# A hybrid streaming-encoder block: part of the depthwise convolution's taps as ScalarE products that accumulating transfers add up

## The chip, the cores and the metric

The kernel runs on one core of one Trainium2 chip. The metric is device time in microseconds (us) of one execution. The kernel before takes 2048.03 us (median of three runs, 2047.39 to 2050.57). One more execution, profiled, took 2048.88 us; the span of its instructions is 2047.1 us. Engines are named as in the profile: PE is TensorE (PEld its weight loads), DVE is VectorE, ACT is ScalarE, POOL is GpSimd, SP is SyncE, which here issues nearly all loads.

## The reference

One layer on a residual stream of 256 tokens by 4096 channels, everything in float32: a projection `xn @ w_in` to 14,336 columns, chunked attention with 16 heads, a Conformer convolution module, gates, an output projection, a gated embedding and a last norm. The change touches the convolution module:

```
u = a * jax.nn.sigmoid(g)
u = jnp.pad(u, ((0, 0), (CONV_K - 1, 0), (0, 0)))          # CONV_K = 31
u = lax.conv_general_dilated(u, w_dw[:, None, :], window_strides=(1,), ...,
                             feature_group_count=CONV_WIDTH) + b_dw
u = jax.nn.silu(layer_norm(u, ln_g, ln_b))
return u @ w_pw + b_pw
```

Each of the 2048 channels has 31 weights of its own. Output token t is the bias plus the sum over k of w[k] times u[t + k - 30].

## The kernel before, in words

**Matrix products.** Both operands of every large product are split into a high and a low part of type fp32r, and three products (high by high, low by high, high by low) are summed in PSUM. A weight tile `wt` holds 128 rows by two runs of 512 columns (512 KB); SP loads it (line 405) into one of five buffers. ACT makes the high part `wh` by a cast (line 204), and DVE then the low part `wl` by a subtraction (line 205); there are three buffers of each. PE multiplies (line 372).

**Units and blocks.** `mixed_product` walks over 16 units of 256 input rows, two weight tiles each; a call with its 16 units is a *block* below. A plain unit has 24 matmuls of 512 columns: 12 for each `wh`/`wl` pair. A unit with a star in the order table uses a seven-product scheme: DVE first forms sums `ua` and `ub` of weight quarters (lines 428 to 433), which ACT and DVE split into `uh` and `ul`; it has 21 matmuls and about three times the DVE work.

**Order of the blocks** (lines 930 to 951): `glu_conv(0)`, `glu_conv(1)`, `keys(0)`, `values(0)`, `attention(0)`, `glu_conv(2)`, `glu_conv(3)`, `keys(1)`, `attention(1)`, `keys(2)`, `layer_norm_swish()`, then two more blocks with the last queries, keys and values. Each `glu_conv(c)` yields one of four channel groups: 512 channels, kept transposed in a tile `uT` of 128 channels by 4 slices by 256 tokens.

**Convolution.** For each group, each of its four slices and each of the 31 taps, one DVE instruction computes `cv = cv + w[k] * (uT shifted)` in place (lines 678 to 685). Tap 30 comes first and also adds the bias; a tap k touches 226 + k tokens. The 124 instructions of a group are put into a queue, `later`. At each unit's end `fill(n)` (lines 182 to 184) takes as many entries from the queue as a table says (`early_fills`, line 325). The queue also holds the layer norm's steps (lines 807 to 822).

**What sets the order.** The recorded order of the program is a priority, not the final order: a scheduler places instructions on each engine as it takes them to be ready, and may move a ready instruction ahead of earlier recorded ones, unless they are pinned (`pin`). Afterwards the order on every engine is fixed: an engine executes its list strictly in that order, and an instruction whose semaphore has not come holds up all behind it on that engine. Tiles of 128 x 4 x 256 floats come from a pool `act` with eight buffers.

Of the kernel before, what the change touches and what calls it, by code (L numbers as in the profile page):

```python
# [10 lines left out]
F32 = mybir.dt.float32  # L11
F32R = mybir.dt.float32r
AF = mybir.ActivationFunctionType
# [12 lines left out]
def hybrid_block(  # L26
# [150 lines left out]
        return [pt[:, i * T : (i + 1) * T] for i in range(len(blocks))]  # L177


    later = deque()  # L180

    def fill(n):
        for _ in range(min(n, len(later))):
            later.popleft()()


    def weight_parts(w, col, k0, kc, tiles=None):
# [134 lines left out]

    valued = units("1 3 5 7 8 0* 9 2* 10 4* 11 6* 12 13 14 15")

    early_fills = (4, 6, 7, 1, 5, 1, 5, 1, 5, 1, 2, 4, 6, 6, 6, 4)
    final = units("1 0* 3 2* 5 4* 6* 7 8* 9 10* 12* 11 13 14 15")
    late = units("1 3 5 7 9 11 13 15 0* 2 4* 6 8* 10* 12 14")

    def mixed_product(
        w, col, lhs, comb, order, on_helpers, ahead=None, fills=(0,), on_begin=None, apart=NB,  # L330
        left=(), begin=None,
    ):

        c = [[ps_acc.tile([P, NB], F32, tag="acc", name=f"acc{h}{j}") for j in range(2)] for h in range(NH)]  # L340
        helper = {}
        begun, ends = set(), {}
        n_left = len(left) // 2
        for n, (_, seven) in enumerate(order[: len(order) - n_left]):
            for name in ("P1", "P5", "P6", "P7", "P2", "P3", "P4") if seven else ("P2", "P3", "P4", "X"):
                ends[name] = n
        banks = {"P2": c[0][0], "P3": c[0][1], "P4": c[1][0], "X": c[1][1]}
        made, held = [], []

        def add_left(h, js, out=None, cols=slice(None)):  # L350


            for m in range(0, len(held), 2):
                for j in js:
                    dst = c[h][j] if out is None else out[:, cols]
                    for i, (kb, (wh, wl)) in enumerate(held[m : m + 2]):
                        xh, xl = block(kb, h)
                        for kind, (a, b) in enumerate(((xh, wh), (xl, wh), (xh, wl))):
                            pin(
                                nc.tensor.matmul(  # L360
                                    dst, a, b[:, j, cols],
                                    start=out is not None and m + i + kind == 0,
                                    stop=m + i + 1 == len(held) and kind == 2,
                                )
                            )

        def add(name, x, w2, n, final, kinds=range(3), then=lambda ins: None):

            for kind in kinds:
                a, b = ((x[0], w2[0]), (x[1], w2[0]), (x[0], w2[1]))[kind]  # L370
                made.append(
                    nc.tensor.matmul(  # L372
                        banks[name], a, b, start=name not in begun,
                        stop=final and ends[name] == n and kind == 2 and not (left and name in "P2 P3 P4"),
                    )
                )
                begun.add(name)
                then(made[-1])

        def block(kb, h):  # L380
            t = lhs[kb // 4]
            return [t[:, kb % 4, q, h * P : (h + 1) * P] for q in range(2)]

        def add_plain(n, k, wh, wl, **kw):
            pair = order[n][0]
            for j in range(2):
                for h in range(NH):
                    name = (("P2", "P3"), ("P4", "X"))[h][j]
                    add(name, block(2 * pair + k, h), (wh[:, j], wl[:, j]), n, k == 1, **kw)

        done, after = 0, ExitStack()
        if begin:
            done, behind = begin(add_plain)
            for ins in behind:
                after.enter_context(tc.issue_after(ins.ins))
        last_seven = max((n for n, (_, seven) in enumerate(order) if seven), default=None)
        for n, (pair, seven) in enumerate(order):
            if n < done:
                continue
            if ahead:  # L400
                ahead(pair)
            wts = []
            for k in range(2):
                wt = wpool.tile([P, 2, NB], F32, tag="w", name="wt")
                nc.sync.dma_start(wt, two_columns(w, 2 * pair + k, col, apart))
                wts.append(wt)
            if n >= len(order) - n_left:
                for k in range(2):
                    tiles = left[2 * (n - len(order) + n_left) + k]
                    held.append((2 * pair + k, parts_of(wts[k], 2, tiles and tiles())[0]))  # L410
                fill(fills[n % len(fills)])
                continue
            if not seven:
                for k in range(2):
                    add_plain(n, k, *parts_of(wts[k], 2)[0])
                fill(fills[n % len(fills)])
                continue
            begins = not helper
            if begins:
                for name in ("P1", "P5", "P7", "P6"):  # L420
                    helper[name] = ps_tmp.tile([P, NB], F32, tag="tmp", name=f"acc_{name}")
                banks.update(helper)
            w0, w1 = wts
            ua = upool.tile([P, 2, NB], F32, tag="u", name="ua")
            ub = upool.tile([P, 2, NB], F32, tag="u", name="ub")
            plus = partial(nc.vector.tensor_tensor, op=ALU.add)
            w0h, w0l = parts_of(w0, 1)[0]
            plus(ua[:, 0], w0[:, 0], w0[:, 1])  # L428
            plus(ua[:, 1], w0[:, 1], w1[:, 1])  # L429
            uah, ual = pair_parts(ua)  # L430
            w1h, w1l = parts_of(w1, 2)[0]
            plus(ub[:, 0], ua[:, 0], w1[:, 1])  # L432
            plus(ub[:, 1], ub[:, 0], w1[:, 0])  # L433
            ubh, ubl = pair_parts(ub)
            first = len(made)

            def s_of(i):
                t, at = comb[pair] if isinstance(comb, dict) else (comb[pair // 4], pair % 4)
                return [t[:, at + i // 2, q, (i % 2) * P : (i % 2 + 1) * P] for q in range(2)]

            k0, k1 = 2 * pair, 2 * pair + 1
            add("P1", block(k0, 0), (w0h[:, 0], w0l[:, 0]), n, True)
            add("P5", s_of(1), (uah[:, 0], ual[:, 0]), n, True)
            add("P7", s_of(0), (uah[:, 1], ual[:, 1]), n, True)
            add("P2", block(k1, 0), (w1h[:, 0], w1l[:, 0]), n, True)
            add("P3", s_of(3), (w1h[:, 1], w1l[:, 1]), n, True)
            add("P6", s_of(2), (ubh[:, 0], ubl[:, 0]), n, True)
            add("P4", block(k1, 1), (ubh[:, 1], ubl[:, 1]), n, True)
            if begins and on_begin:
                on_begin()  # L450
            if begins:
                tc.add_manual_dep(
                    made[first].ins, last_transpose[0].ins.name,
                    mybir.DependencyInfo(mybir.DependencyClass.NoSync, mybir.DependencyReason.DATA),
                    reason="transposes before the helpers take their banks",
                )
            if n == last_seven:
                on_helpers(helper)
            fill(fills[n % len(fills)])
        after.close()  # L460
        return (c, add_left) if left else c

# [210 lines left out]

    conv = []

    def conv_tap(cv, uT, i, b, k):
        if k == PAD:
            nc.vector.tensor_scalar(
# [2 lines left out]
        else:  # L681
            nc.vector.scalar_tensor_tensor(  # L682
                cv[:, i, PAD - k :], uT[:, i, : T + k - PAD], dw[:, b, k : k + 1],
                cv[:, i, PAD - k :], ALU.mult, ALU.add,
            )

    def more_combinations(pair):

# [5 lines left out]
    def glu_conv(c):  # L694
# [4 lines left out]
        else:  # L699
            last = c == CW // NB - 1  # L700
            sg, gate = scaled_pair(
                w_in0, o_a + c * NB, o_g - o_a, early_six if last else early, r_x, early_fills,
                ahead=more_combinations if last else None,
            )
        for h in range(NH):
# [15 lines left out]
            )  # L721
        cv = act.tile([P, 4, T], F32, tag="act", name="cv")
        for i in range(4):
            for k in reversed(range(TAPS)):
                later.append(partial(conv_tap, cv, uT, i, 4 * c + i, k))
        conv.append(cv)


# [185 lines left out]
    def keys(g, fills):  # L914
        q, k = blocks((o_q + g * NB, o_k + g * NB), early, fills)
        queries(g, q)
        keyed(g, k)
# [4 lines left out]
    def late_pool():  # L922
# [13 lines left out]
    glu_conv(2)  # L936
    glu_conv(3)
    load_bias(1)
    keys(1, early_fills)
    attention(1)  # L940
    keys(2, early_fills)
    layer_norm_swish()
    load_bias(2)
    q, vs[2] = blocks((o_q + 3 * NB, o_v + 2 * NB), early, (4,))
    queries(3, q)
    attention(2)
    k, vs[3] = blocks(
        (o_k + 3 * NB, o_v + 3 * NB), valued, (5, 5, 4, 5, 4, 2, 3, 2, 3, 2, 3, 4, 4, 4, 4, 4),
        then=late_pool,
    )  # L950
    keyed(3, k)
# [358 lines left out]
```

## Time and profile before

| | before |
|---|---|
| median of the runs | 2048.03 us |
| profiled execution | 2048.88 us, span 2047.1 us |
| busy share PE / DVE / ACT / POOL | 99% / 95% / 58% / 0% |
| granted TensorE clock, mean | 0.996 |
| DMA traffic | 412.30 MB, mean 201 GB/s |
| convolution's taps (DVE) | from 105.9 us to 805.1 us of the span |

A row of groups reads: line, engine, operation, what it writes and reads, shape and count, then busy time, mean duration in ns, idle time just before. Matmuls are pipelined: the recorded duration of a matmul is longer than its distance to the next one, so a busy PE is not necessarily a PE at its peak. A row of windows gives busy time and count of each engine in a stretch of the span. A row of the chain of waits gives a start, a length and whose work it was.

### The profile page before, as it was taken

Reading aid. Unit: us, or ns where it says so; the run is one execution under the profiler, and the core shown is the slowest. Engines: PE = TensorE matmul, PEld = TensorE weight load, DVE = VectorE, ACT = ScalarE, POOL = GpSimd, SP = SyncE. Lnnn points to the kernel's source line nnn. Section 1 sums busy time; section 2 is a strip of 40 time slices with the busy share of each in tenths; the row PEclk is TensorE's granted clock in tenths of the full one; section 3 lists DMA queues with packets and bytes.
Section 4 is the critical chain, followed back from the end, with each engine's and each line's share of the span. In section 5 each row is a group of like instructions: output and inputs, shape, how many; then the busy total and the mean of one; then the engine's idle time right before and its main releaser. Section 6 shows DMA issues by size and latency. Waiting matters only on the chain.

```text
span 2047.1 us, 26034 instructions
## 1 busy us (share of the span) xinstructions
PE 2022.0 (99%) x9082; PEld 1656.1 (81%) x9082; DVE 1943.8 (95%) x2784; ACT 1195.2 (58%) x1543; POOL 8.1 (0%) x19
## 2 busy tenths in 40 slices
PE   9999999999999999999999999999999999999997
PEld 7888888888778888878888888888888888888876
DVE  7999999989999999889899999999999999999998
ACT  7655545655555544676565656676565666655555
POOL 0000000000000000000000000000000000000000
PEclk9999999999999999999999999999999999999998
DMA  8666666566665666645666666676666656666765
GB/s 288 192 197 205 204 192 200 165 203 185 192 187 170 199 198 183 191 155 199 192 213 210 193 214 200 216 242 208 214 198 206 204 188 208 199 220 205 235 207 179
DMA packets 157758, 412.30 MB, mean 201 GB/s; under 512 B 12974, under 2 KB 16190, under 8 KB 157626
## 3 DMA queue, kind: packets, MB, share of 16 engines
q1 hardware_dynamic: 156976, 409.80, 63.5%
q8 instruction: 71, 1.16, 0.2%
q10 hardware_dynamic: 650, 0.84, 0.1%
q14 instruction: 61, 0.50, 0.1%
HBM read 406.39 MB, written 4.19 MB: 201 GB/s over the span
## 4 chain that ended last, share of the span: by engine, by line
PE 88%; DVE 7%; issue 2%; DMA 1%; ACT 1%; SPq 0%; POOL 0%; POOLq 0%; ACTq 0%; DVEq 0%
PE acc L372 69%; PE acc_P L372 16%; DVE wl L205 2%; DVE cv L682 2%; PE tmp_ps L170 1%; DVE ul L205 1%; PE acc L218 1%; DMA wt<-in_w_in_dram 1%; DVE ub L433 0%; PE tmp_ps L835 0%; PE tmp_ps L851 0%; DVE ub L432 0%; DMA wt<-in_w_out_dram 0%; ACT wh L204 0%; PE tmp_ps L869 0%
## 5 line engine op out<-in xcount | busy, mean ns | idle before, releaser
L372 PE MATMUL acc<-wh,big_t 128*128 128x512 f32 x4196 | 1296.9, 392 | 2.5 <-ACT wh L204 1.0
L204 ACT CAST wh<-wt 128x1024 fp32r<-128x1024 f32 (+1 forms) x737 | 711.1, 976 | 561.0 <-PE acc L372 416.2
L372 PEld LDWEIGHTS acc<-wh,big_t 128*128 128x128 f32 x4196 | 784.9, 188 | 166.3 <-ACT wh L204 1.8
L205 DVE TENSOR_TENSOR wl<-wt,wh 128x1024 fp32r<-128x1024 f32 (+1 forms) x737 | 819.5, 1123 | 36.6 <-ACT wh L204 32.4
L372 PE MATMUL acc<-wl,big_t 128*128 128x512 f32 x2098 | 805.6, 392 | 2.8 <-DVE wl L205 2.7
L372 PEld LDWEIGHTS acc<-wl,big_t 128*128 128x128 f32 x2098 | 393.4, 188 | 87.8 <-DVE wl L205 6.1
L682 DVE SCALAR_TENSOR_TENSOR cv<-uT,dw,cv 128x255 f32<-128x255 f32 (+22 forms) x480 | 212.1, 460 | 1.0
L204 ACT CAST uh<-ub 128x1024 fp32r<-128x1024 f32 x130 | 136.7, 1052 | 114.0 <-DVE ub L433 97.4
L204 ACT CAST uh<-ua 128x1024 fp32r<-128x1024 f32 x130 | 136.9, 1053 | 82.2 <-DVE ua L429 76.5
L205 DVE TENSOR_TENSOR ul<-ub,uh 128x1024 fp32r<-128x1024 f32 x130 | 158.4, 1219 | 7.0 <-ACT uh L204 6.3
L372 PE MATMUL acc_P<-uh,big_t 128*128 128x512 f32 x528 | 161.6, 393 | 0.0
L205 DVE TENSOR_TENSOR ul<-ua,uh 128x1024 fp32r<-128x1024 f32 x130 | 158.3, 1218 | 0.8 <-ACT uh L204 0.2
L372 PEld LDWEIGHTS acc_P<-uh,big_t 128*128 128x128 f32 x528 | 97.4, 188 | 24.3 <-ACT uh L204 5.1
L428 DVE TENSOR_TENSOR ua<-wt 128x512 f32<-128x512 f32 x130 | 89.0, 685 | 18.1 <-DMA wt<-in_w_in_dram 11.4
L372 PE MATMUL acc_P<-ul,big_t 128*128 128x512 f32 x264 | 101.1, 394 | 1.2 <-DVE ul L205 1.2
L429 DVE TENSOR_TENSOR ua<-wt 128x512 f32<-128x512 f32 x130 | 88.7, 683 | 1.8 <-DMA wt<-in_w_in_dram 1.1
L433 DVE TENSOR_TENSOR ub<-ub,wt 128x512 f32<-128x512 f32 x130 | 88.9, 684 | 0.9
L432 DVE TENSOR_TENSOR ub<-ua,wt 128x512 f32<-128x512 f32 x130 | 88.7, 683 | 0.3
L372 PE MATMUL acc<-uh,big_t 128*128 128x512 f32 x260 | 80.6, 390 | 0.0
L372 PE MATMUL acc_P<-wh,big_t 128*128 128x512 f32 x260 | 80.4, 389 | 0.0
L372 PE MATMUL acc_P<-uh,comb_t 128*128 128x512 f32 x228 | 69.8, 391 | 0.1
L372 PEld LDWEIGHTS acc_P<-ul,big_t 128*128 128x128 f32 x264 | 49.2, 188 | 15.2 <-DVE ul L205 5.0
(240 smaller groups left out, 1370.1 us busy)
## 6 DMA issues: line engine op xcount, KB each, us to landing
wt<-in_w_in_dram SPq DMA_DIRECT2D x447, 512.0 KB, 4.2
wt<-in_w_out_dram SPq DMA_DIRECT2D x128, 512.0 KB, 4.1
wt<-in_w_ple_gate_dram SPq DMA_DIRECT2D x128, 512.0 KB, 4.2
wt<-in_w_pw_dram SPq DMA_DIRECT2D x32, 512.0 KB, 4.5
hc<-in_x_dram SPq DMA_DIRECT2D x8, 512.0 KB, 5.8
wt<-in_w_ple_dram SPq DMA_DIRECT2D x8, 512.0 KB, 4.5
xin<-in_x_dram SPq DMA_DIRECT2D x7, 512.0 KB, 7.9
out_dram<-hc SPq DMA_DIRECT2D x12, 256.0 KB, 2.8
```

Of the source, the lines that this page charges most:

```text
L170: nc.tensor.transpose(pt[:, i * T + h * P : i * T + (h + 1) * P], src[:, h, b] if len(src.shape) == 4 else src[:, h, b * P : (b + 1) * P], ...
L204: nc.scalar.copy(wh[:, :kc, :], wt[:, :kc, :]),
L205: nc.vector.tensor_tensor(wl[:, :kc, :], wt[:, :kc, :], wh[:, :kc, :].bitcast(F32), ALU.subtract),
L218: nc.tensor.matmul(acc, a, b[:, k, :], start=kb == 0 and kind == 0, stop=kb == kblocks - 1 and kind == 2,)
L372: nc.tensor.matmul(banks[name], a, b, start=name not in begun, stop=final and ends[name] == n and kind == 2 and not (left and name in "P2 ...
L428: plus(ua[:, 0], w0[:, 0], w0[:, 1])
L429: plus(ua[:, 1], w0[:, 1], w1[:, 1])
L432: plus(ub[:, 0], ua[:, 0], w1[:, 1])
L433: plus(ub[:, 1], ub[:, 0], w1[:, 0])
L682: nc.vector.scalar_tensor_tensor(cv[:, i, PAD - k :], uT[:, i, : T + k - PAD], dw[:, b, k : k + 1], cv[:, i, PAD - k :], ALU.mult, ALU.add,)
```

## The change

For each group the lowest taps (k = 0 to 14 of the first two groups, 0 to 13 of the third, 0 to 9 of the fourth: 54 taps) leave DVE. Such a tap becomes four ACT products, one per slice, from `uT` into a tile `tap`, whose first 30 tokens POOL sets to zero once; then POOL issues one transfer of 512 KB that adds the whole tile onto `cv` (`accum_op=ALU.add`). A group has two `tap` tiles, used in turn. The adds of a group are put into a second queue, `adds`, behind the group's remaining DVE taps; `add_one` takes one of them at two of three units. Those that are left are recorded ahead of `layer_norm_swish`. The tables of `fill` are changed to fit the shorter queue.

```
+    def add_one(n):
+        if adds and n % 3 < 2:
+            adds.popleft()()
...
-    early_fills = (4, 6, 7, 1, 5, 1, 5, 1, 5, 1, 2, 4, 6, 6, 6, 4)
+    early_fills = (4, 5, 5, 1, 4, 1, 4, 1, 4, 1, 2, 3, 4, 4, 4, 3)
+    more_fills = (6, 7, 7, 2, 6, 2, 6, 2, 6, 2, 4, 6, 8, 8, 8, 6)
...
             fill(fills[n % len(fills)])
+            add_one(n)
...
+    ADDED = (15, 15, 14, 10)
+
+    def conv_added(cv, uT, c):
+
+        held = []
+
+        def tap(k):
+            if k < 2:
+                held.append(act.tile([P, 4, T], F32, tag="act", name="tap"))
+                nc.gpsimd.memset(held[k][:, :, :PAD], 0.0)
+            t = held[k % 2]
+            for i in range(4):
+                b = 4 * c + i
+                nc.scalar.activation(
+                    t[:, i, PAD - k :], uT[:, i, : T + k - PAD], AF.Identity,
+                    scale=dw[:, b, k : k + 1],
+                )
+            nc.gpsimd.dma_start(cv, t, accum_op=ALU.add)
+
+        return [partial(tap, k) for k in range(ADDED[c])]
...
         for i in range(4):
-            for k in reversed(range(TAPS)):
+            for k in reversed(range(ADDED[c], TAPS)):
                 later.append(partial(conv_tap, cv, uT, i, 4 * c + i, k))
+        later.append(lambda: adds.extend(conv_added(cv, uT, c)))
...
-    keys(1, early_fills)
+    keys(1, more_fills)
     attention(1)
     keys(2, early_fills)
+    while adds:
+        adds.popleft()()
     layer_norm_swish()
     load_bias(2)
-    q, vs[2] = blocks((o_q + 3 * NB, o_v + 2 * NB), early, (4,))
+    q, vs[2] = blocks((o_q + 3 * NB, o_v + 2 * NB), early, (3,))
```

(`more_fills` also serves the block of `glu_conv(3)`; the table of the last block goes from 3 to 5 entries a unit to one a unit and then none until its twelfth unit.)

**How it stands on ACT.** Before, in the first units of `keys(0)`, ACT's list holds only the casts of weights (`wh`) and weight sums (`uh`):

```order
L204 CAST wh<-wt 128x1024 [waits DMAHW0_49,DVE_49,PE_49]
L204 CAST wh<-wt 128x1024 [waits DVE_49,DMAHW1_49,PE_49,Activation_49]
L204 CAST wh<-wt 128x1024 [waits DMAHW2_49,DVE_49,PE_49]
L204 CAST wh<-wt 128x1024 [waits DMAHW4_49,DVE_49,PE_49]
L204 CAST uh<-ua 128x1024 [waits DVE_49]
L204 CAST wh<-wt 128x512 [waits DMAHW5_49,PE_49,Activation_49]
L204 CAST wh<-wt 128x1024 [waits DMAHW6_49,PE_49,Activation_49]
```

After the change the same place reads as follows. `DMASWn` is the semaphore by which a transfer of POOL tells that it has landed; the number at the end of a shape tells the tap (226 + k).

```order
L208 CAST wh<-wt 128x1024 [waits DMAHW2_49,DVE_49,PE_49]
L707 ACTIVATE tap<-uT,dw 128x229 [waits DMASW1_49,Activation_49]
L707 ACTIVATE tap<-uT,dw 128x229 [waits Activation_49]
L208 CAST uh<-ua 128x1024 [waits DVE_49]
L707 ACTIVATE tap<-uT,dw 128x229 [waits Activation_49]
L208 CAST wh<-wt 128x1024 [waits DMAHW4_49,PE_49]
L707 ACTIVATE tap<-uT,dw 128x229 [waits Activation_49]
L707 ACTIVATE tap<-uT,dw 128x230 [waits DMASW2_49]
L707 ACTIVATE tap<-uT,dw 128x230 x2
L208 CAST wh<-wt 128x512 [waits DMAHW5_49,PE_49,Activation_49]
L707 ACTIVATE tap<-uT,dw 128x230
```

The products of tap k + 2 write the tile that the transfer of tap k reads, so they wait for its landing, and casts of weights stand behind them. Although one add is recorded at two of three units, the scheduler has placed the first group's products from tap 2 to tap 14 within the casts of about ten units.

**How it stands on POOL.** Before, POOL's list in this part of the program holds a few settings of bias tiles:

```order
L139 TENSOR_TENSOR r_x<-r_x,mhalf 128x2 [waits DVE_49,Pool_49]
L901 MEMSET bias 64x4x64 [waits DMAHW3_49]
L901 MEMSET bias 64x4x64 [waits DMAHW5_49,DMAHW3_49,DMAHW7_49,DVE_49,PE_49]
```

After the change the adds of the first group stand there, each behind the landing of the one before it, since all write the same `cv`:

```order
L711 DMA cv<-tap 128x1024 [waits DMAHW2_49,DMAHW4_49,DVE_49,DMAHW5_49,Activation_49,Pool_49]
L703 MEMSET tap 128x4x30 [waits DMAHW7_49,PE_49]
L931 MEMSET bias 64x4x64 [waits DMAHW3_49]
L711 DMA cv<-tap 128x1024 [waits DMASW0_49,Activation_49,Pool_49]
L711 DMA cv<-tap 128x1024 [waits DMASW1_49]
L711 DMA cv<-tap 128x1024 [waits DMASW2_49,Activation_49]
L711 DMA cv<-tap 128x1024 [waits DMASW3_49,Activation_49]
```

The first of them waits for the last DVE tap of its group; the others form a chain of single transfers.

More of the change, by code (lines that the diff above doesn't have):

```diff
@@ L177, in transposed @@
         return [pt[:, i * T : (i + 1) * T] for i in range(len(blocks))]
-    later = deque()
+    later, adds = deque(), deque()
     def fill(n):
@@ L459, in mixed_product @@
             fill(fills[n % len(fills)])
+            add_one(n)
         after.close()
@@ L701, in glu_conv @@
             sg, gate = scaled_pair(
-                w_in0, o_a + c * NB, o_g - o_a, early_six if last else early, r_x, early_fills,
+                w_in0, o_a + c * NB, o_g - o_a, early_six if last else early, r_x,
+                more_fills if last else early_fills,
                 ahead=more_combinations if last else None,
@@ L947, in hybrid_block @@
     k, vs[3] = blocks(
-        (o_k + 3 * NB, o_v + 3 * NB), valued, (5, 5, 4, 5, 4, 2, 3, 2, 3, 2, 3, 4, 4, 4, 4, 4),
+        (o_k + 3 * NB, o_v + 3 * NB), valued, (1, 1, 1, 1, 1, 1, 1, 0, 0, 0, 0, 4, 4, 4, 4, 4),
         then=late_pool,
```

## The prediction

> **What bounds the kernel now.** I read the page's first part first, for the engines and the traffic:
>
> ```profile
> PE 2022.0 (99%) x9082; PEld 1656.1 (81%) x9082; DVE 1943.8 (95%) x2784; ACT 1195.2 (58%) x1543; POOL 8.1 (0%) x19
> PE 88%; DVE 7%; issue 2%; DMA 1%; ACT 1%; SPq 0%; POOL 0%; POOLq 0%; ACTq 0%; DVEq 0%
> q1 hardware_dynamic: 156976, 409.80, 63.5%
> ```
>
> PE is nearly always at work, and the chain that ended last is PE's for 88%, DVE's for 7%. So how much can freeing DVE give at all? The windows show the stretch of the convolution and the one behind it:
>
> ```profile
> 100.00:830.00 730.00, 725.24 (x3263) 591.33 (x3262) 713.86 (x1138) 380.24 (x465) 0.92 (x3) 1.00 0.63 190
> 830.00:1010.00 180.00, 175.67 (x790) 142.43 (x789) 160.02 (x262) 116.63 (x185) 2.47 (x4) 0.99 0.58 184
> ```
>
> The columns are PE, PEld, DVE, ACT, POOL, clock, DMA share, GB/s. In the first stretch DVE works 713.86 of 730 us: it has no room, and PE no visible gap. But recorded matmuls overlap, so I count them instead. An unbroken piece of the chain gives the true pace, and the groups of PE in 100 to 830 us give the small shapes (first and last of eight groups, 235 matmuls together):
>
> ```profile
> 329.73 27.88 PE acc L372 x123
> ...
> L835 PE MATMUL tmp_ps<-ident,z 128*128 128x128 f32 x56 | 8.2, 276 | 0.0
> ...
> L874 PE MATMUL tmp_ps<-z,pT 128*128 128x128 f32 x22 | 4.2, 272 | 0.0
> ```
>
> 27.88 / 123 = 0.2267 us per matmul of 512 columns. 3263 - 235 = 3028 such matmuls need 686.5 us; the small ones I put at 0.11 us each (estimate, between a quarter of 0.2267 and the recorded 0.272), 26 us. That leaves 730 - 712 = 18 us in which PE starves. The same count for 830 to 1010 us, whose groups of small shapes (first and last of nine) hold 79 of the 790 matmuls, gives 711 x 0.2267 + 79 x 0.11 = 170 of 180 us and leaves 10:
>
> ```profile
> L869 PE MATMUL tmp_ps<-ident,s 128*128 128x128 f32 x15 | 3.5, 287 | 0.9 <-ACT s L862 0.9
> ...
> L748 PE MATMUL tmp_ps<-lnsum,mean_w 128*128 128x256 f32 x2 | 0.6, 380 | 0.0
> ```
>
> So **28 us is the ceiling** of what a free DVE can return, whatever it is relieved of. The cover that every stall must get through is small.
>
> **The change part by part.**
>
> *Removed: 216 DVE taps* (4 x (15 + 15 + 14 + 10)).
>
> ```profile
> L682 DVE SCALAR_TENSOR_TENSOR cv<-uT,dw,cv 128x240 f32<-128x240 f32 x16 | 7.4, 460 | 0.1
> ...
> L682 DVE SCALAR_TENSOR_TENSOR cv<-uT,dw,cv 128x226 f32<-128x226 f32 x16 | 7.1, 446 | 0.0
> ```
>
> 216 x 0.453 = 98 us of DVE work, far more than PE lacks. Bounds of the gain: 0 and 28 us. I take 15: about two thirds of the 18, a little of the 10, because attention's short chains and the seven-product units keep their own waits. The new fill tables only move taps between blocks; the densest, `keys(1)` with 84 taps instead of 64, gains 20 x 0.453 = 9 us of DVE work, the blocks around it lose more. I take nothing for that, with up to 9 us lost as its bound.
>
> *Added on ACT: 216 products* of 128 x 226 to 240 from SBUF to SBUF. The trace has no such product; the nearest rows, with the casts that they stand among:
>
> ```profile
> L204 ACT CAST wh<-wt 128x1024 fp32r<-128x1024 f32 x607 | 630.9, 1052 | 476.0 <-PE acc L372 362.9 <-DVE cv L682 18.4 <-ACT uh L204 15.6
> L204 ACT CAST wh<-wt 128x512 fp32r<-128x512 f32 x130 | 80.7, 620 | 85.0 <-PE acc L372 53.3 <-issue 12.1 <-ACT wh L204 9.1
> L492 ACT ACTIVATE z<-z,r_x 128x512 f32<-128x512 f32 x30 | 20.6, 717 | 12.6 <-DVE z L471 11.0 <-DVE z L473 1.5
> L862 ACT ACTIVATE s<-s,nm 128x256 f32<-128x256 f32 x16 | 7.9, 494 | 0.0
> L862 ACT ACTIVATE s<-s,nm 128x128 f32<-128x128 f32 x16 | 6.4, 401 | 11.0 <-DVE nm L861 11.0
> ```
>
> Between 0.40 and 0.494 us; I take 0.47, so 1.9 us a tap and 101 us in all. ACT works 380 of 730 us in the stretch, so on the average there is room. What counts is where the products stand.
>
> *Added wait.* The products of tap k + 2 wait for the landing of tap k's add, and the adds of one group wait for each other. Behind a waiting product stand casts of weights; behind a cast stands DVE's `wl`, and behind that PE. So I compare the chain of adds with the matmuls whose casts stand among the products. From the products of tap 2 to those of the last tap the list of the changed kernel holds 26, 25, 22 and 12 casts in the four groups. A plain `wh` feeds 12 matmuls, the parts of a seven-product unit 3, 6, 6 and 6; that is 204, 198, 174 and 96 matmuls, **46.2, 44.9, 39.4 and 21.8 us, 152 us together**. In the same time the chain must land n - 2 adds: 13, 13, 12 and 8, **46 landings**. PE thus leaves 3.3 us a landing, plus a head start: at the moment of a group's last DVE tap two to three weight tiles are cast or ready to be (12 x 0.2267 = 2.7 us each), 7 us a group; the fourth group lies beside `attention(1)`, whose small matmuls I put at 5 us. In sum the chain costs PE
>
> 46 L - (152 + 28 + 5) = 46 L - 185 us, where L is the time from an add's issue to its landing.
>
> With the 15 us of relief the change breaks even at **L = 200 / 46 = 4.35 us**.
>
> *What is L?* No transfer in the trace adds, goes from SBUF to SBUF or is issued by POOL. The nearest rows are loads and stores:
>
> ```profile
> wt<-in_w_in_dram SPq DMA_DIRECT2D x447, 512.0 KB, 4.2
> xin<-in_x_dram SPq DMA_DIRECT2D x7, 512.0 KB, 7.9
> out_dram<-hc SPq DMA_DIRECT2D x12, 256.0 KB, 2.8
> gin_rows<-in_norm_in_g_dram SPq DMA_DIRECT2D x1, 16.0 KB, 2.1
> ```
>
> A tiny load takes 2.1 us, a 512 KB weight tile 4.2, the start's crowded loads 7.9. By the queue's row, 63.5% of 2047.1 us for 409.80 MB is 1.66 us of all 16 engines per 512 KB. An add must read `cv` as well as `tap`, so it moves between one and two times that: 2.1 + 1.7 = 3.8 us and 2.1 + 3.3 = 5.4 us on an idle set of engines. The set is not idle: weights use 0.63 of it in the stretch, which can stretch the transfer's own part by up to that share, to 4.8 and 7.5 us. Lower end 3.6 us (the store of 256 KB and another 0.8 for the rest), upper end 7.5. I take **5.5**, nearest to a weight tile's 4.2 plus most of a second read; that is the choice on which the forecast hangs.
>
> The Trainium skill, page "DMA: Bandwidth & Descriptors", section "Anatomy of one DMA — SWDGE (gpsimd) path", gives a transfer issued by GpSimd as 2.0 us plus its bytes at 436 GB/s: estimated from it, 3.2 us for 512 KB, and the sum would have no stall at all. Its page "Collectives: The Full Stack", section "The bandwidth ceiling: the fold count and why AG ≠ RS ≠ AR", says that an addition within a transfer needs two source reads on one ring and halves the rate; with that the estimate is 4.4 us, the break-even itself. No transfer of this trace tests either.
>
> *Weights.* Added traffic is 54 x 512 KB, 28 MB beside some 139 MB of the stretch. SP issues a weight tile when a buffer comes free, mostly long before it is needed:
>
> ```profile
> SPq L405 <- DVE wl L205: 1046.3, 470, 9.8
> ```
>
> SP waits for buffers, and DMA holds 1% of the chain; with five buffers and 2.7 us of PE a tile, a tile that lands 5 us later should still be in time (estimate). Cost nothing, and a loss only if the DMA engines fill up (a rival below). POOL's memsets of `tap` and bias stand between adds; their loads are issued well ahead: nothing.
>
> *Sum.* 46 x 5.5 - 185 = +68; relief -15; **+53 us** on the profiled 2048.9: 2102, on the median, 0.85 lower, some **2100 us**.
>
> **The rivals.**
>
> *The adds land in 4 us or less.* Then the chain stays ahead of the casts, and only the relief is left: 2048 - 15 = 2033, from 2026 to 2043. For it speaks that the idle-set bound with one read is 3.8 us and that a stalled PE asks for fewer weights; against it, that every 512 KB load in the trace, with one read, takes 4.2 or more. It decides for L below 4.25. By the first rule of the Trainium skill above this is the result. Chance 0.33.
>
> *ACT itself becomes the limit.* From tap 2 to the last tap ACT's own work in the four groups is 85 casts, 83 us, plus 168 products at 0.47, 79 us, plus 7 us of attention: 169 us against 152 + 5 us of PE's. Even with instant adds, ACT falls behind by some 12 us and the relief is eaten up: 2046 to 2051. It needs L of about 4.0 to 4.4 or a product dearer than 0.47. For it: ACT has to do 48 us in the first group's 46. Against: the head start of 7 us a group covers it. Chance 0.08.
>
> *The DMA engines fill up.* At two reads an add takes 3.3 us of all engines; one each 5.5 us is 0.6 of the set on top of the weights' 0.63. Then loads of weights come late as well and L passes 7: 46 x 7 - 200 = +122, 2170 us and more. For it: the two shares exceed one. Against: a PE that stalls asks for less. Chance 0.12.
>
> *The forecast,* a chain of adds at 4.8 to 6.9 us that holds ACT and so PE: chance 0.47, own range 2069 to 2165.
>
> **How the numbers follow.** A difference under 0.2%, 4 us, cannot be told from none. Faster is the first rival, 0.33; same the second, 0.08; slower the forecast and the third, 0.59. The range of 8 in 10 goes from the fast case's 2026 to the forecast's upper end, 2165, since cases of both signs hold most of the chance.
>
> **What would show it.** Right: in the changed profile ACT's products of taps wait for DMA landings, 1 us and more each; casts behind them are late and PE idles for ACT's `wh` and DVE's `wl` by tens of us, all in four stretches of 45 to 75 us between 190 and 830 us; the issues of `cv<-tap` take about 5.5 us to land. DVE's busy time falls by about 98 us, ACT's rises by about 100. Wrong: landings under 4.2 us, no waits of ACT for them, and the span shorter by 10 to 20 us. Wrong in another way: PE waiting for loads of `wt`, or products far from 0.47 us.

## The result: 5.6% slower, and the profile after

| | before | after |
|---|---|---|
| median | 2047.71 us (four runs) | 2163.53 us (four runs, 2160.82 to 2167.07) |
| ratio | | 1.0564, 95% interval 1.0551 to 1.0577 |
| profiled execution, span | 2048.88, 2047.1 us | 2167.07, 2165.3 us |
| granted TensorE clock, mean | 0.996 | 0.977 |

The change costs 116 us. The forecast was +53, with the same sign and the same mechanism. The time lies inside the range only just, 1.5 us under its upper end of 2165, and the loss is more than twice the one forecast. What follows asks for the missing 63 us.

First the same rows as before, from the page after: engines, shares of the chain that ended last, the two queues that matter (`q0` carries POOL's adds), and the adds' row among the issues.

```profile
PE 2061.7 (95%) x9082; PEld 1674.4 (77%) x9082; DVE 1872.1 (86%) x2568; ACT 1276.1 (59%) x1759; POOL 56.7 (3%) x81
q1 hardware_dynamic: 156976, 409.80, 59.1%
q0 software_dynamic: 7776, 28.32, 7.1%
PE 57%; DMA 5%; DVE 4%; issue 2%; ACT 1%; POOLq 0%; POOL 0%; ACTq 0%; DVEq 0%
cv<-tap POOLq DMA_DIRECT2D x54, 512.0 KB, 5.5
```

DVE is relieved as intended, and PE's busy share falls from 99% to 95%. The shares of the chain must not be set beside those before: the chain after could be followed back only to 654 us of the span, so its shares add up to 69% and leave out the first two groups. What it does show is DMA's 5% (1% before), of which the adds hold 3%. The windows after, cut at the four stretches in which adds are issued (length, then PE, PEld, DVE, ACT, POOL, clock, DMA share, GB/s), show where PE lost:

```profile
180.00:280.00 100.00, 81.22 (x312) 62.13 (x311) 69.61 (x102) 58.38 (x100) 14.05 (x19) 0.88 0.86 216
280.00:400.00 120.00, 98.08 (x386) 75.21 (x385) 72.92 (x95) 64.57 (x106) 13.21 (x16) 0.89 0.79 209
400.00:600.00 200.00, 192.60 (x852) 154.72 (x851) 164.75 (x240) 106.01 (x136) 0.00 (x0) 0.99 0.58 177
600.00:710.00 110.00, 87.89 (x338) 66.56 (x337) 81.38 (x127) 62.26 (x101) 13.09 (x18) 0.91 0.80 206
710.00:800.00 90.00, 75.63 (x338) 60.90 (x337) 62.99 (x104) 50.53 (x98) 8.67 (x10) 0.92 0.73 190
```

The same time in the kernel before:

```profile
180.00:400.00 220.00, 220.00 (x1003) 181.67 (x1002) 218.50 (x357) 116.86 (x144) 0.31 (x1) 1.00 0.63 191
400.00:600.00 200.00, 195.84 (x849) 157.38 (x849) 191.83 (x293) 105.38 (x118) 0.30 (x1) 0.99 0.63 191
```

In the first two stretches there are 698 matmuls in 220 us, where the kernel before does 1003. Between 400 and 600 us, where no add runs, PE does 852, about as many as before. No engine is full in the four bad stretches: DVE 70%, ACT 58%, PE 81% in the first. The waits say who waits for whom (sum in us, count, longest):

```profile
ACT tap L707 <- DMA cv<-tap: 127.8, 43, 7.3
DVE wl L209 <- ACT wh L208: 126.9, 101, 7.1
PE acc L377 <- ACT wh L208: 42.8, 13, 6.5
POOL cv L711 <- DMA cv<-tap: 66.7, 12, 8.7
DVE ua L434 <- DMA wt<-in_w_in_dram: 30.4, 23, 3.6
```

Read from top to bottom this is the predicted sequence: products wait for landings, weight casts stand behind the products, DVE's `wl` waits for the casts, PE waits for both (for `wl` 11.9 us, by the page's groups). One instance of it, on ACT's timeline after (start, length; in brackets the idle time before and who ended it):

```profile
244.82 1.25 ACT L707 ACTIVATE tap<-uT,dw 128x236 f32<-128x236 f32 x3 [3.04 <-DMA cv<-tap]
245.98 1.03 ACT L208 CAST uh<-ub 128x1024 fp32r<-128x1024 f32 x1
246.91 0.49 ACT L707 ACTIVATE tap<-uT,dw 128x236 f32<-128x236 f32 x1
247.30 1.03 ACT L208 CAST wh<-wt 128x1024 fp32r<-128x1024 f32 x1
```

and what PE does meanwhile:

```profile
243.50 0.39 PE L377 MATMUL acc_P<-ul,big_t 128*128 128x512 f32 x1
248.39 1.22 PE L377 MATMUL acc<-wh,big_t 128*128 128x512 f32 x2 [4.49 <-ACT wh L208]
...
250.24 1.05 PE L377 MATMUL acc<-wh,big_t 128*128 128x512 f32 x2
251.09 0.63 PE L377 MATMUL acc<-wl,big_t 128*128 128x512 f32 x1
```

ACT sits still for 3.04 us before tap 10's products. The cast at 247.30 starts without idle time of its own, behind the products and another cast, and PE idles 4.49 us until it is done. The last two rows show something that the prediction did not have: two matmuls from 250.24 to 251.09 are 0.425 us apart, not 0.227. The windows for these microseconds give the granted clock:

```profile
248.50:252.50 4.00, 3.96 (x9) 2.66 (x10) 2.67 (x4) 2.48 (x5) 0.86 (x1) 0.50 0.66 154
255.00:260.00 5.00, 5.00 (x23) 4.12 (x23) 3.51 (x6) 2.17 (x5) 0.88 (x1) 1.00 1.00 278
```

After the idle gap PE runs at half clock for some microseconds (9 matmuls in 4 us), then at full clock again (23 in 5 us).

The adds themselves, on POOL's timeline after:

```profile
208.39 0.89 POOL L711 DMA_DIRECT2D cv<-tap  x1 [5.25 <-DMA cv<-tap]
213.87 0.87 POOL L711 DMA_DIRECT2D cv<-tap  x1 [4.59 <-ACT tap L707]
219.23 0.86 POOL L711 DMA_DIRECT2D cv<-tap  x1 [4.49 <-ACT tap L707]
227.86 0.86 POOL L711 DMA_DIRECT2D cv<-tap  x1 [7.77 <-ACT tap L707]
```

Their landing time, as the view of line 711 gives it:

```profile
DMA to landing us min/median/max: 4.5/5.5/9.8
```

The median is the 5.5 us that the prediction took, but the mean over all 54 is 5.88, since the distribution reaches to 9.8. And within a group the issues of this piece are 5.4 to 8.6 us apart; over 49 of the 50 such distances, all but one of 17.7 us at the third group's start, the mean is 6.45. Where POOL had nothing else to wait for, the next issue starts 0.64 us after the landing (counted from the landing to the start of the next issue, median). That hand-off was in no term of the sum.

### The profile page after: what moved, and what is told of

Read it like the earlier page. It is cut to its first block, busy times and chain, and to the rows that moved or that the text cites. A ratio compares the mean times of both kernels' runs of the same rounds, so it can differ in the third digit from the quotient of the medians.

```text
span 2165.3 us, 26257 instructions
## 1 busy us (share of the span) xinstructions
PE 2061.7 (95%) x9082; PEld 1674.4 (77%) x9082; DVE 1872.1 (86%) x2568; ACT 1276.1 (59%) x1759; POOL 56.7 (3%) x81
## 4 chain that ended last, share of the span: by engine, by line
PE 57%; DMA 5%; DVE 4%; issue 2%; ACT 1%; POOLq 0%; POOL 0%; ACTq 0%; DVEq 0%
PE acc L377 43%; PE acc_P L377 11%; DMA cv<-tap 3%; DVE wl L209 2%; DMA wt<-in_w_in_dram 1%; DMA wt<-in_w_out_dram 1%; PE acc L222 1%; DVE cv L691 1%; PE tmp_ps L170 1%; ACT wh L208 1%; DVE ul L209 0%; ACT tap L707 0%; DMA wt<-in_w_ple_gate_dram 0%; PE acc L365 0%; DVE ub L438 0%
## 5 line engine op out<-in xcount | busy, mean ns | idle before, releaser
L377 PE MATMUL acc<-wh,big_t 128*128 128x512 f32 x4196 | 1310.5, 395 | 43.2 <-ACT wh L208 42.8
L377 PE MATMUL acc<-wl,big_t 128*128 128x512 f32 x2098 | 813.2, 395 | 12.1 <-DVE wl L209 11.9
L707 ACT ACTIVATE tap<-uT,dw 128x226 f32<-128x226 f32 (+14 forms) x216 | 92.3, 480 | 127.8 <-DMA cv<-tap 127.8
L691 DVE SCALAR_TENSOR_TENSOR cv<-uT,dw,cv 128x255 f32<-128x255 f32 (+16 forms) x264 | 117.1, 469 | 0.3
```

Of the source, the lines that this page charges most:

```text
L377: nc.tensor.matmul(banks[name], a, b, start=name not in begun, stop=final and ends[name] == n and kind == 2 and not (left and name in "P2 ...
L691: nc.vector.scalar_tensor_tensor(cv[:, i, PAD - k :], uT[:, i, : T + k - PAD], dw[:, b, k : k + 1], cv[:, i, PAD - k :], ALU.mult, ALU.add,)
L707: nc.scalar.activation(t[:, i, PAD - k :], uT[:, i, : T + k - PAD], AF.Identity, scale=dw[:, b, k : k + 1],)
```

## The experiments

All of them are compared with the kernel before; its medians beside them lay between 2047.77 and 2048.07 us. Each is the changed kernel with the edit shown. Below, kernel 6 is the kernel of experiment 6, and so on.

**1. Is it the hold of ACT by the chain?** The products are pinned to where the program records them, two taps in three units, so that they no longer crowd into ten units.

```
-                nc.scalar.activation(
+                pin(nc.scalar.activation(
                     t[:, i, PAD - k :], uT[:, i, : T + k - PAD], AF.Identity,
                     scale=dw[:, b, k : k + 1],
-                )
+                ))
```

> Edit: the products of the taps stay where they are recorded on ACT (pinned behind the casts of their unit); transfers, products and counts unchanged. Between a group's tap 2 and its last tap ACT's list now holds casts for 49 to 91 us of matmuls, 7.0 to 7.5 us a tap, instead of 3.1 to 3.9. Theory (the chain of adds, 5.9 us a landing plus 0.64 us to the next issue, holds ACT because the products stand too early): 6.5 us a tap now fits, ACT's waits for adds fall from 127.8 us to under 40, the time to 2035 to 2060 us. Rival (the added traffic or ACT's added work slows the stretch wherever it stands): more than 2100 us, with PE waiting as before.

Measured: 2096.69 us, ratio 1.0230 (1.0197 to 1.0262); the four runs lie between 2086.56 and 2102.61 us, and the profile is of the slowest. 67 of the 116 us are gone, more than the rival allowed and less than the theory wanted. The waits of this kernel:

```profile
DVE wl L209 <- ACT wh L208: 95.1, 83, 7.6
DVE ua L434 <- DMA wt<-in_w_in_dram: 44.8, 28, 4.2
ACT tap L707 <- DMA cv<-tap: 40.1, 16, 5.7
```

ACT's waits for adds fell from 127.8 to 40.1 us with the transfers all still there. So the place of the products in ACT's list decides most of the loss. The pin also spreads the adds: from a group's first issue to its last, summed over the groups, it takes 451 us instead of 334; what part of the 67 us that gives, this run does not separate. DVE's waits for weights stay high. The same row of the waits in the kernel before:

```profile
DVE ua L428 <- DMA wt<-in_w_in_dram: 11.4, 15, 1.9
```

44.8 us against 11.4. Most of that rise needs no transfer, for kernel 6, which has neither products nor adds, already has:

```profile
DVE ua L434 <- DMA wt<-in_w_in_dram: 28.4, 23, 2.9
```

As I read it, DVE with fewer taps reaches `ua` sooner and waits there longer. 16 us stand above that, so something is left that the hold does not explain.

**2. The second read.** The transfer copies instead of adding. The sum of the taps is left out by that: `cv` ends as the last product tile.

```
-            nc.gpsimd.dma_start(cv, t, accum_op=ALU.add)
+            nc.gpsimd.dma_start(cv, t)
```

> Edit: the 54 transfers copy the product onto cv instead of adding it (cv ends as the last product alone); same chain, same waits, same sizes. If the second read is what makes an add dearer than a 512 KB load, landings fall from a median of 5.5 us to about 4.2 and the mean pace from 6.5 to about 5.2 us: 46 landings x 1.3 = 60 us less, about 2105 us. If the landing is fixed cost and contention with the weights, landings stay at 5 us and more and the time at 2145 to 2165 us.

Measured: 2107.00 us, 1.0280 (1.0259 to 1.0302). The queue and the issues of this kernel:

```profile
q0 software_dynamic: 7776, 28.32, 3.5%
cv<-tap POOLq DMA_DIRECT2D x54, 512.0 KB, 4.3
```

The same packets and bytes take 3.5% of 16 engines' span instead of 7.1%: 0.035 x 2098.0 / 54 = 1.36 us of all engines for one transfer, against 0.071 x 2165.3 / 54 = 2.85 us for an add. An add costs the engines twice a copy, the landing median falls from 5.5 to 4.3 us, and 57 of the 116 us go. They are not all due to the earlier landing: by experiments 9 and 10, lighter traffic alone would give 54 x (0.61 - 0.24) = 20 of them.

**3. More tiles.** Four `tap` tiles instead of two in the first two groups, so that products wait for the add of tap k - 4.

```
-            if k < 2:
+            if k < (4 if c < 2 else 2):
...
-            t = held[k % 2]
+            t = held[k % (4 if c < 2 else 2)]
```

> Edit: four tap tiles instead of two in the first two groups, so ACT's products may run four adds ahead of the chain instead of two; everything else as in the change. Theory (ACT is held by the chain, pace 6.5 us a landing): the last products of these groups wait for 11 landings instead of 13, 2 x 2 x 6.5 = 26 us less, while the casts among them shrink from 91 to 79 us of matmuls, 12 us back: 14 us less than the changed kernel's 2163.5, 2145 to 2155 us. Rival (contention by the transfers themselves, no matter who waits): no difference, 2160 us or more.

Measured: 2156.70 us, 1.0528 (1.0512 to 1.0544): 7 us less, between the two ranges and half of the middle of the theory's. As I read it, a deeper buffer only delays the moment at which the products meet the chain; the adds still go one behind the other.

**4. Two halves.** Each add as two of 256 KB, so that the two can overlap.

```
-            nc.gpsimd.dma_start(cv, t, accum_op=ALU.add)
+            for j in (0, 2):
+                nc.gpsimd.dma_start(cv[:, j : j + 2], t[:, j : j + 2], accum_op=ALU.add)
```

> Edit: each add becomes two transfers of 256 KB, slices 0 and 1 and slices 2 and 3, which form two chains beside each other. Theory: a landing of 5.9 us is some 2.6 us of fixed time and 3.3 us of transfer; two chains overlap the fixed part, and the pace falls from 6.5 to about 5.4 us: 46 x 1.1 = 51 us less, while the scheduler puts the products among 18 us less of matmuls: 2120 to 2140 us. If the transfer's own part or POOL's issuing (0.87 us each, now twice as many) sets the pace: 2155 to 2190 us.

Measured: 2159.52 us, 1.0543 (1.0527 to 1.0558); the rival was right. The issues:

```profile
cv<-tap POOLq DMA_DIRECT2D x108, 256.0 KB, 5.1
```

A half takes 5.1 us where the whole takes 5.5. With the halves issued side by side, splitting does not shorten the chain.

**5. Products alone.** The transfers are left out, and with them the sum of the 54 taps.

```
-            nc.gpsimd.dma_start(cv, t, accum_op=ALU.add)
```

> Edit: the 54 adding transfers are left out, so those taps are missing from the convolution; ACT still makes all 216 products. Theory (chain of adds): nothing holds ACT any more, 2030 to 2048 us. Rival (ACT's own work of 101 us is the limit, 169 us of it against 157 us of matmuls in four stretches): 2060 us or more, most of the loss stays.

Measured: 2052.14 us, 1.0020 (1.0010 to 1.0030), between the two ranges. ACT's 216 products are nearly free. But the time is not below that of the kernel before, though DVE has 216 taps less: the relief is missing. That led to 6 and 7.

**6. The relief alone.** The 54 taps are computed nowhere.

```
-        later.append(lambda: adds.extend(conv_added(cv, uT, c)))
```

> Edit: the 54 taps of ADDED are computed nowhere (products and adds left out), with DVE's 280 remaining taps and the fill tables as in the change. It measures the relief of DVE alone. The forecast's 15 us: 2030 to 2036 us. The counted ceiling of 28 us: 2020 us. If it stays above 2043 us, freeing DVE was worth almost nothing, and no placement of the adds could win.

Measured: 2050.45 us, 1.0010 (1.0000 to 1.0019). With these fill tables, even taking 216 instructions from DVE for nothing gains nothing. The products thus cost 2052.14 - 2050.45 = 2 us.

**7. The relief with the old table.** As 6, with the fill table of the kernel before in the blocks that got the dense one.

```
-    more_fills = (6, 7, 7, 2, 6, 2, 6, 2, 6, 2, 4, 6, 8, 8, 8, 6)
+    more_fills = (4, 6, 7, 1, 5, 1, 5, 1, 5, 1, 2, 4, 6, 6, 6, 4)
```

> Edit: as the kernel with the 54 taps left out (2050.5 us), but the blocks of glu_conv(3) and keys(1) take the old table of 64 entries a block instead of 86. If the relief of DVE is real and the denser table ate it in these two blocks (PE idles some 10 us more there than before), 2040 to 2046 us. If freeing DVE was worth nothing anywhere because PE did not wait for DVE's throughput, 2047 to 2052 us.

Measured: 2040.30 us, 0.9961 (0.9946 to 0.9976), as expected. The relief is there, 8 us, and the dense table takes 10 us away again. Three rows of windows show the place. Kernel 6 with the dense table:

```profile
400.00:600.00 200.00, 190.01 (x815) 150.71 (x814) 182.09 (x276) 100.64 (x111) 0.31 (x1) 0.99 0.60 182
```

kernel 7 with the old one:

```profile
400.00:600.00 200.00, 195.25 (x847) 156.92 (x845) 183.61 (x270) 105.81 (x118) 0.30 (x1) 0.99 0.63 190
830.00:1010.00 180.00, 179.34 (x814) 147.09 (x813) 153.03 (x229) 106.41 (x162) 2.25 (x2) 1.00 0.60 192
```

In 400 to 600 us, the blocks of `glu_conv(3)` and `keys(1)`, the dense table costs 847 - 815 = 32 matmuls, 32 x 0.2267 = 7 us. The gain stands behind the convolution: from 830 to 1010 us PE does 814 matmuls where the kernel before did 790, about 5 of the 8 us.

**8. The change with the old table.** The edit of 7, with all taps and adds.

> Edit: the change with the old table of 64 entries in the blocks of glu_conv(3) and keys(1). Theory: the denser table's 10 us go (2050.45 to 2040.3 us without adds), and the scheduler now places the products of the last two groups among 14 us more of matmuls: 24 us less than 2163.5, 2134 to 2150 us. If the chain alone decides and the table is hidden behind it: 2155 to 2167 us.

Measured: 2149.69 us, 1.0501 (1.0483 to 1.0518): 14 us less than the change, at the upper end of the theory's range; kernel 7 explains 10 of them.

**9. The traffic alone.** Products as in the change, and beside them 50 adding transfers of the same size and shape from `uT` into a spare tile, for which neither ACT nor DVE nor PE waits. The sum of the 54 taps is left out.

```
-                nc.gpsimd.memset(held[k][:, :, :PAD], 0.0)
-            t = held[k % 2]
+                nc.gpsimd.memset(held[k] if k else held[k][:, :, :PAD], 0.0)
+            t = held[0]
...
-            nc.gpsimd.dma_start(cv, t, accum_op=ALU.add)
+            if k:
+                nc.gpsimd.dma_start(held[1], uT, accum_op=ALU.add)
```

> Edit: all products are made, and 50 adding transfers of 512 KB run, each waiting for the one before, but from uT onto a spare tile that nobody reads: no product waits for an add, and no add for a product (the 54 taps are missing from the convolution). It has the traffic of the chain without its hold on ACT. Theory (the hold is the cost): within 10 us of the kernel with products alone (2052 us), 2050 to 2062 us. Rival (the transfers slow the weight loads and so DVE and PE): 2080 us or more.

Measured: 2082.65 us, 1.0172 (1.0155 to 1.0189). The rival was right: transfers that hold nobody cost 2082.65 - 2052.14 = 30.5 us over kernel 5, 0.61 us each. Kernel 5, the stretch of the first two groups:

```profile
180.00:400.00 220.00, 218.05 (x988) 178.63 (x988) 184.53 (x258) 145.38 (x230) 0.79 (x4) 1.00 0.61 189
```

and its waits for weights:

```profile
DVE ua L434 <- DMA wt<-in_w_in_dram: 32.3, 25, 2.9
```

and the same two views of the kernel with the traffic:

```profile
180.00:400.00 220.00, 205.84 (x912) 165.97 (x911) 172.66 (x245) 125.31 (x187) 24.98 (x31) 0.98 0.90 241
```

```profile
DVE ua L434 <- DMA wt<-in_w_in_dram: 52.6, 28, 5.8
```

The landings of the weight loads in this stretch (line 410), first without and then with the traffic:

```profile
DMA to landing us min/median/max: 3.3/3.9/6.2
DMA to landing us min/median/max: 3.7/5.8/8.5
```

The DMA share rises from 0.61 to 0.90, loads of weights land 1.9 us later as a median, DVE waits 20 us longer for them, and PE does 76 matmuls fewer in the 220 us. The adds themselves land at a median of 6.8 us here, against 5.5 in the change, where PE stalls and less is loaded (241 GB/s here, 216 and less there).

**10. The same traffic as copies.** As 9, without `accum_op`.

```
-                nc.gpsimd.dma_start(held[1], uT, accum_op=ALU.add)
+                nc.gpsimd.dma_start(held[1], uT)
```

> Edit: as the run with the traffic apart (2082.65 us), but the 50 transfers copy instead of adding. A packet of 4 KB took 160 ns as a copy and 339 ns as an add, 1.36 against 2.84 us of all 16 engines a transfer. Theory (the loads of weights come late because the DMA engines are busy): the 30 us above the products alone fall to a half or less, 2055 to 2069 us. If it is the number of transfers or POOL's work on descriptors that disturbs: 2077 to 2087 us.

Measured: 2064.37 us, 1.0088 (1.0070 to 1.0106). The cost of the traffic falls from 30.5 to 12 us, and the engines' time per transfer from 2.91 us (7.0% of 2077.6 us over 50) to 1.32 us:

```profile
q0 software_dynamic: 7200, 26.22, 3.2%
tap<-uT POOLq DMA_DIRECT2D x50, 512.0 KB, 5.0
```

0.24 us lost per transfer against 0.61, 1.32 us of engines against 2.91: the loss goes about with the engines' time, not with the number of transfers.

**11. Half as many.** 8, 8, 7 and 5 taps are taken from DVE instead of 15, 15, 14 and 10.

```
-    ADDED = (15, 15, 14, 10)
+    ADDED = (8, 8, 7, 5)
```

> Edit: ADDED is 8, 8, 7, 5 (28 adds instead of 54; DVE keeps the other 104 taps), placement by the scheduler as in the change. Theory (a chain that must land n - 2 adds while ACT's list covers little matmul time): 20 landings x 6.5 us against 53 us of matmuls among the products, 28 us of head start and 5 us of attention leaves 44 us on a base of 2050 us: 2085 to 2102 us. If instead each add costs its share of the measured 113 us (28 of 54, 59 us): 2104 to 2115 us.

Measured: 2104.46 us, 1.0277 (1.0262 to 1.0293): 57 us for 28 adds, 116 for 54, about 2.1 us an add in both; the loss by the share of the adds was right. The theory, the prediction's formula with a pace of 6.5 us, gave 44 us over the 2050 of kernel 6, where 54 were measured. This dose is not free either.

**12. Half as many, spread out.** As 11, pinned as in 1, and at one of three units.

```
-        if adds and n % 3 < 2:
+        if adds and n % 3 < 1:
```

> Edit: 28 adds (8, 8, 7, 5), recorded at one unit of three, the products kept where they are recorded; 13 to 15 us of matmuls a tap, twice the pace of the chain, but for the last group's flush. Theory: no hold is left, only the traffic of the transfers (30 us for 50 of them when they ran apart, 0.6 us each, 17 us): 2060 to 2070 us. If sparse transfers hide beside the weights: 2046 to 2055 us. If ACT is still held: 2075 us or more.

Measured: 2069.25 us, 1.0105 (1.0090 to 1.0120). The waits:

```profile
ACT tap L707 <- DMA cv<-tap: 7.4, 2, 5.0
```

Of ACT's waits for adds only two are left, and so are 21 us for 28 adds, 0.77 us each. That lies near the price of the traffic, but the run does not show that the traffic is the cause: the dense table, worth 10 us in 7, is in it too, and PE's longest wait stands behind an idle DVE in the fourth group's stretch:

```profile
754.81 1.29 DVE L870 COPY qT<-tmp_ps 128x512 f32<-128x512 f32 x2 [8.05 <-issue]
758.42 0.80 PE L377 MATMUL acc<-wl,big_t 128*128 128x512 f32 x1 [5.55 <-DVE wl L209]
```

None of the runs that compute every tap beats the kernel before. What freeing DVE of all 54 taps returns, 8 us (7), is less than the traffic of their adds, 54 x 0.61 = 33 us (9); so I see no placement of these adds that could. Few adds, spread out and with the old table, were not run.

## Why the prediction was right and where it was wrong

Put together, the 116 us divide about so. This takes the parts as adding up, which the runs make plausible and do not prove:

| part | from | us |
|---|---|---|
| relief of DVE, old table | 2040.30 - 2048 | -8 |
| dense fill table | 2050.45 - 2040.30 | +10 |
| ACT's products | 2052.14 - 2050.45 | +2 |
| traffic of 54 adds | 54 x 0.61 | +33 |
| hold of ACT by the chain | the rest | +79 |

The hold's 79 us and, in a small part, the traffic's 33 contain the time that PE ran at half clock (below).

**The step that failed is in the sum's sizes, not in its mechanism.** The sum had +68 for the hold, -15 for the relief, and nothing for products, tables and traffic. By the runs the relief with its new tables is +2 (6), the products +2 (5), the traffic +33 (9), and 79 are left for the hold. So the missing 63 us are 33 of traffic, 17 of relief, 11 of hold and 2 of products. The relief is measured by itself. The other 46 us can be booked otherwise, as a chain with a slower pace (the paragraph on L below), since late landings slow both; the two accounts describe the same time and do not add up.

**Right.** The sign, the mechanism and its place. Products of taps wait 43 times, 3.0 us on average; PE starves in four stretches while adds are issued (92, 89, 93 and 59 us long from the first issue to the last, where 45 to 75 us was said). Most of the hold goes when the products stand elsewhere with all transfers in place (1), and time falls when the transfers land sooner (2), though there the traffic is lighter too. The rival of adds that land in 4 us or less falls: none of the 54 took under 4.5.

**"ACT products 0.47 us each".** The row after:

```profile
L707 ACT ACTIVATE tap<-uT,dw 128x226 f32<-128x226 f32 (+14 forms) x216 | 92.3, 480 | 127.8 <-DMA cv<-tap 127.8
L691 DVE SCALAR_TENSOR_TENSOR cv<-uT,dw,cv 128x255 f32<-128x255 f32 (+16 forms) x264 | 117.1, 469 | 0.3
```

480 ns recorded, and three in 1.25 us on the timeline above, so 0.39 us apart: ACT's room was even larger, and the rival that ACT itself is the limit falls (2 us, experiments 5 and 6).

**"216 x 0.453 = 98 us of DVE work".** The group of taps before, beside the last row above:

```profile
L682 DVE SCALAR_TENSOR_TENSOR cv<-uT,dw,cv 128x255 f32<-128x255 f32 (+22 forms) x480 | 212.1, 460 | 1.0
```

The taps fell by 212.1 - 117.1 = 95 us, yet DVE's busy time only by 1943.8 - 1872.1 = 72. Recorded DVE instructions overlap their neighbours, as matmuls do (at 242.48 us DVE's timeline after has five taps in 2.01 us, 0.39 us apart, where 469 ns is the recorded mean), and I had corrected that for PE alone. It moved no time here, since DVE's relief was bounded by PE's gap.

**"L = 5.5 us", a term that was mis-sized.** 46 L - 185 comes near if L is the pace and not the landing: mean landing 5.88 plus 0.64 to the next issue is 6.52, and 46 x 6.52 - 185 = 115 us, against 2163.53 - 2050.45 = 113 over the kernel without the taps. For the copies of experiment 2, mean landing 4.46 and the same hand-off, it gives 46 x 5.10 - 185 = 50 against 2107.00 - 2050.45 = 57. A chain is paid by the mean, and I had put in a median; and each link has a hand-off that I had left at nothing. The two together, 46 x (6.52 - 5.5) = 47 us, are by this account the larger part of the missing 63. That the formula fits the change so closely is partly luck: with half the taps it gave 44 us where 54 were measured (11), four tiles gained half of what it gave (3), and it holds neither the traffic's cost to the weights nor the half clock (both below).

**"Relief taken 15 us" and the fill tables "nothing ... with up to 9 us lost as its bound".** With the new tables the relief is +2.5 - that is, none (6); with the old one it is 8 us, and the table costs 10 (7), the bound itself and a little more. The 28 us ceiling was a count of PE's gaps and right as a ceiling; but of the 18 us before 830 us next to nothing came back, though DVE was free, so most of those gaps were not due to the taps. This term makes 17 of the 63 us (from -15 to +2).

**Weights: "cost nothing, and a loss only if the DMA engines fill up".** The engines did not fill up on the average (0.73 to 0.86 in the four stretches), L never reached the 7 us of that rival as a mean, and the traffic still cost about 33 us (9). The step that failed is "a tile that lands 5 us later should still be in time": the row of SP's waits was read as slack for every tile, while DVE's `ua` of the seven-product units already waited 11.4 us for weights before the change. Those waits are the row that should have shown that some tiles have no slack, and in 9 landings 1.9 us later were enough. So this rival had a part in the result without its condition, and the split between it and the hold is blurred by the formula, which books late landings as hold.

The Trainium skill, page "DMA: Bandwidth & Descriptors", section "Anatomy of one DMA — SWDGE (gpsimd) path", from which 3.2 us was estimated, is far off for adds beside weight loads: 4.5 us is the fastest of 54. Copies of the same size take 4.3 us as a median, with 2.9 as the fastest (2). Its page "Collectives: The Full Stack", section "The bandwidth ceiling: the fold count and why AG ≠ RS ≠ AR", says of a collective's add that it needs two source reads on one ring and halves the rate; the trace agrees as to the factor, 2.85 against 1.36 us of all engines, and does not show the reads.

## What to carry to other kernels

A chain of dependent transfers is paid link by link, at the mean landing plus the hand-off to the next issue, and it holds up everything that is queued behind it on the engine that feeds it; so compare its pace with the work that stands among its links before counting what it relieves. An adding transfer took the DMA engines twice the time of a copy (2.85 against 1.36 us), and beside weight loads with a DMA share of 0.61 it made loads late even where nobody waited for it. Before moving work off an engine that looks full, leave that work out altogether: if the kernel does not get faster by more than the new place can cost, no placement will help, and here that run gained 8 us at best.

## What the runs showed of the hardware that I had not expected

**Half clock behind idle gaps.** With gaps of a few microseconds PE ran at a granted clock of 0.50 (rows above), matmuls 0.425 us apart. In the clock's record such stretches come in multiples of 3.4 us and add up, start and end of the kernel left out, to 92 us after, in 16 stretches, against 7 us before; the 118 matmuls in them lost about 22 us (counted as each one's distance to the next, beyond 0.227). In experiment 1 it is 27 us of such stretches and 6 us lost. In the change PE has 16 idle gaps of over 2 us, the shortest 2.3 and the longest 6.9 us, and within 5 us of the start of each begins one of the stretches. So some 20 of the 116 us are not waiting but slow running behind a wait. No run tested this cost by itself. The Trainium skill, page "TensorE: Matmul & The Clock Gate", section "HAM oscillation — how this bites in real kernels", warns of gaps of over 3.4 us for this reason. The trace agrees for the longer half of the 16 (4.49 us idle, then 0.50), but the other eight are 2.3 to 3.4 us long, so here shorter gaps were enough. The prediction should have weighed it, since it forecast waits of this size.

**The split add.** Two adds of 256 KB side by side take 5.1 us each to land, one of 512 KB takes 5.5. Whether a half alone would be quicker was not tried.

**What stays open.** How much of the 79 us of hold is the chain's own pace and how much is landings stretched by the weights' traffic, which is the same contention seen from the other side. The runs take away the one or the other, but the kernel has both. Open too is what a few spread adds cost with the old table.
